# Splitting two output stores into 8-row transfers, and one group for the last four values of the last unit

## Chip, cores and metric

The kernel runs on one core of one Trainium2 chip. The metric is device time in microseconds (us), lower is better. Run-to-run spread is given beside each median.

## The reference

```python
batch, n_heads, seq, head_dim = 8, 12, 1024, 64
attn_weights: (8, 12, 1024, 1024) float32
v:            (8, 12, 1024, 64)   float32
out = np.einsum('bhqs,bhsd->bhqd', attn_weights, v)
```

Reading the weights in float32 is nearly all of the traffic: 402.7 MB of them, 25.2 MB of `v`, and 25.2 MB written.

## The kernel before

The 96 heads are worked off in 48 pairs ("units"). For each unit, GpSimd (POOL) issues one load of 128 rows that converts float32 to bf16 on the way. PE (the matmul engine) transposes the weights, multiplies by `v`, and transposes the result back; DVE (VectorE) and ACT (ScalarE) do the copies between; the output unit (128 rows of 4 KB) is stored by a transfer that POOL issues. Two weight buffers let the next load run during compute. The stores of the seven units before the last are held back and issued behind the last load ("held stores" below). Shortened, with comments of mine:

```python
def load_attn(ip):                       # one unit = 128 rows of 64 KB in float32
    abf = abf_pool.tile([P, G, S], bf16)             # two buffers
    for g0, gn in chunks_of.get(ip, [(0, G)]):       # last units: in parts
        last = nc.gpsimd.dma_start(out=abf[:, ds(g0, gn)]..., in_=attn_p[ip][...])

def store(ip, osb):
    nc.gpsimd.dma_start(
        out=out_p[ip].rearrange("p g d -> p (g d)"),     # 128 rows of 4 KB
        in_=osb.rearrange("p g d -> p (g d)"),
        single_packet=True,
    )

# the last unit: parts of 4, 4, 4, 2, 1 and 1 of its 16 values, each part
# transposed, multiplied, copied out, and stored on its own from SP
chunks_of[NP - 1] = [(0, 4), (4, 4), (8, 4), (12, 2), (14, 1), (15, 1)]
stores_of = {4: (0, 8), 8: (8, 4), 12: (12, 2), 15: (14, 2)}

# ... (transposes, multiplications and the copies between them are cut)
```

## Time and profile before

| | before |
|---|---|
| time, median of 4 runs | 1061.61 us (1061.13 to 1061.64) |
| span in the profile | 1059.6 us |
| DMA engines busy | 90% or more in 39 of 40 slices |
| PE busy | 76% |
| last load landed / last small store issued | 1048.6 / 1054.29 us |
| last held store, completion on its first / last DMA engine | 1050.1 / 1057.8 us |

From the page of the kernel before: the share of the span in 40 slices (tenths, so 9 is 90% or more), the DMA queues, the total of the memory traffic, and the chain that ended last.

```profile
DMA  9999999999999999999999999999999999999998
...
q0 software_dynamic: 18432, 238.03, 100.0%
q1 hardware_dynamic: 720, 1.57, 0.4%
q8 instruction: 44, 0.72, 0.2%
q14 instruction: 12, 0.10, 0.0%
HBM read 427.82 MB, written 25.17 MB: 428 GB/s over the span
...
DMA 73%; issue 14%; PE 9%; POOL 2%; ACT 1%; DVE 0%; POOLq 0%
```

The kernel is bound by DMA: the DMA engines have hardly any idle time to remove. q1 is the queue of the transfers that SP (SyncE) issues. q8 holds 44 packets of 16 KB (16384 bytes in the packet records) of the kind that the page calls instruction: 0.72 MB of 240 (the records count a 64 KB row of weights by the 32 KB that it writes as bf16), 0.2% of the time of 16 engines. The list of waits says the same from PE's side (columns: who waited for what, us in total, times, longest):

```profile
PE pt L150 <- DMA abf<-in_attn_weights_dram: 194.3, 49, 24.9
```

The trace keeps 16 landing times for every load of weights. I read them as one for each of the 16 DMA engines that the page counts; which engine a time belongs to is not recorded. They show what the 16-engine mean hides. Times in us after the first of the 16, sorted, for a load of weights (landing records of the trace, not a view of the page):

```
first landed at   the other engines behind it
  24.58   0.0 0.0 0.0 0.0 0.0 0.1 0.1 0.1 0.1 0.1 0.1 0.1 0.1 0.1 0.1 0.2
 220.41   0.0 0.0 0.1 0.1 0.2 0.4 0.4 0.6 1.3 1.3 1.3 1.3 1.4 1.4 1.6 1.9
 612.76   0.0 0.0 0.1 0.2 0.4 0.5 1.0 1.6 3.5 3.5 3.5 3.6 3.6 3.7 3.8 4.0
1035.53   0.0 0.1 0.1 0.2 0.4 0.8 1.8 2.8 5.8 5.8 5.8 5.9 6.0 6.9 7.1 7.3
```

Eight engines fall behind, in steps of about 1.1 us, one engine after another, at the times of the 16 KB instruction packets (for one, a delay of 1.4 us in the load first landed at 396.04 us is 2.4 in the load at 415.33, and a packet started at 411.6). What waits for a load waits for the slowest engine: of the load in the last row the first landing is at 1035.53 us and the last at 1042.86, and PE starts its transposes at 1042.99. So the time of this kernel is that of its slowest engine.

The end of the last unit, in the timeline of the kernel before (start us, duration us, engine and line, operation, count, and in brackets the idle time ahead and what ended it):

```profile
1042.95 11.67 SPq L266 DMA_DIRECT2D out_dram<-osb  x4
...
1042.99 2.17 PE L150 MATMUL pt<-ident,abf 128*128 128x128 f32 x16 [0.92 <-DMA abf<-in_attn_weights_dram]
...
1046.79 1.18 PE L150 MATMUL pt<-ident,abf 128*128 128x128 f32 x8
...
1049.33 0.70 PE L150 MATMUL pt<-ident,abf 128*128 128x128 f32 x4
...
1051.66 0.70 PE L150 MATMUL pt<-ident,abf 128*128 128x128 f32 x4
...
1053.15 0.62 PE L252 MATMUL px<-vbf,at 128*128 128x128 bf16 x8 [0.79 <-DVE at L159]
...
1054.06 0.21 ACT L263 COPY osb<-px 64x64 f32<-64x64 f32 x1 [1.74 <-DVE osb L263]
```

The last four values go through in three groups (8, 4 and 4 transposes), each waiting for its own copies.

### The profile page before, as it was taken

The page shows a single profiled execution, that of the slowest core. Times are in us where ns is not written, and L with a number is a line of the kernel's source. Part 1 is how long each engine was busy: PE and PEld are TensorE (multiplying, and loading weights), DVE is VectorE, ACT ScalarE, POOL GpSimd, SP SyncE. Part 2 cuts the span into 40 slices and gives each one's busy share as a digit, 9 for nine tenths or more (in the row PEclk, how much of TensorE's full clock was granted, in tenths as well). Part 3 has the DMA queues.
Part 4 walks back from the last instruction along what each step waited for, and adds up shares of the span by engine and source line. Part 5 has one row for each costly group of instructions (what it writes and reads, how often), then busy time and mean ns, then how long its engine had stood idle before and what let it go on. Part 6 is the DMA issues. An engine that isn't in the chain of part 4 may idle for free.

```text
span 1059.6 us, 12899 instructions
## 1 busy us (share of the span) xinstructions
PE 808.4 (76%) x5640; PEld 645.0 (61%) x5640; DVE 390.7 (37%) x590; ACT 399.6 (38%) x486; POOL 71.8 (7%) x137
## 2 busy tenths in 40 slices
PE   0988778876778767787687876888678776788996
PEld 0676567654666556665476655766557555676785
DVE  0443334433344333343334333343334333344443
ACT  0353334433344333344344333443334333343542
POOL 2000000000000000000000000000000000001011
PEclk9998878988888888788888887788889887788999
DMA  9999999999999999999999999999999999999998
GB/s 217 219 218 234 222 237 231 225 226 222 239 224 232 222 231 237 223 220 231 238 226 229 227 224 236 229 222 229 229 230 235 221 227 228 236 215 210 217 215 243
DMA packets 19208, 240.43 MB, mean 227 GB/s; under 512 B 2128, under 2 KB 2512, under 8 KB 11984
## 3 DMA queue, kind: packets, MB, share of 16 engines
q0 software_dynamic: 18432, 238.03, 100.0%
q1 hardware_dynamic: 720, 1.57, 0.4%
q8 instruction: 44, 0.72, 0.2%
q14 instruction: 12, 0.10, 0.0%
HBM read 427.82 MB, written 25.17 MB: 428 GB/s over the span
## 4 chain that ended last, share of the span: by engine, by line
DMA 73%; issue 14%; PE 9%; POOL 2%; ACT 1%; DVE 0%; POOLq 0%
DMA abf<-in_attn_weights_dram 73%; PE pt L150 5%; PE px L186 2%; ACT osb L194 1%; POOL vr L124 1%; POOL out_dram L203 1%; PE px L136 1%; PE px L252 1%; PE po L169 0%; DVE vbf L144 0%; POOL abf L108 0%; DVE at L159 0%; ACT at L159 0%; DVE osb L263 0%; ACT osb L263 0%
## 5 line engine op out<-in xcount | busy, mean ns | idle before, releaser
L150 PE MATMUL pt<-ident,abf 128*128 128x128 f32 x3072 | 463.2, 319 | 194.3 <-DMA abf<-in_attn_weights_dram 194.3
L150 PEld LDWEIGHTS pt<-ident,abf 128*128 128x128 f32 x3072 | 449.7, 214 | 209.4 <-issue 116.3
L159 DVE COPY at<-pt 128x1024 bf16<-128x1024 bf16 x480 | 319.5, 688 | 443.1 <-PE pt L150 441.7
L159 ACT COPY at<-pt 128x1024 bf16<-128x1024 bf16 x288 | 288.7, 1012 | 223.3 <-PE pt L150 129.2
L169 PE MATMUL po<-at,vbf 128*64 128x512 bf16 x1440 | 216.5, 391 | 0.0
L169 PEld LDWEIGHTS <-vbf 128*64 128x64 bf16 x1440 | 106.5, 108 | 92.9
L194 ACT COPY osb<-px 128x512 f32<-128x512 f32 x90 | 50.8, 587 | 154.9 <-PE px L186 151.5
L181 ACT COPY ot<-po 128x512 f32<-128x512 f32 x45 | 26.3, 585 | 191.4 <-PE po L169 191.4
L186 PE MATMUL px<-ident,ot 128*128 128x128 f32 x360 | 69.8, 340 | 30.3 <-DVE vbf L144 17.4
L186 PEld LDWEIGHTS px<-ident,ot 128*128 128x128 f32 x360 | 52.8, 174 | 50.7 <-DVE vbf L144 28.7
L144 DVE CAST vbf<-px 128x512 bf16<-128x512 f32 x48 | 33.2, 691 | 95.9 <-PE px L136 95.9
L181 DVE COPY ot<-po 128x512 f32<-128x512 f32 x45 | 31.1, 691 | 100.8 <-PE po L169 100.8
L136 PE MATMUL px<-vr,spread 32*128 32x512 bf16 x384 | 53.8, 386 | 18.5 <-DVE vbf L144 18.5
L108 POOL DMA_DIRECT2D abf<-in_attn_weights_dram x58 | 31.5, 546 | 512.5 <-PE pt L150 507.2
L203 POOL DMA_DIRECT2D out_dram<-osb x47 | 25.2, 536 | 462.8 <-ACT osb L194 424.8
L144 ACT CAST vbf<-px 128x512 bf16<-128x512 f32 x48 | 28.1, 585 | 63.7 <-PE px L136 63.7
L136 PEld LDWEIGHTS <-spread 32*128 32x128 bf16 x384 | 17.2, 93 | 52.5 <-issue 43.0
L252 PE MATMUL px<-vbf,at 128*128 128x128 bf16 x384 | 23.9, 219 | 2.3 <-ACT at L159 1.2
L252 PEld LDWEIGHTS <-at 128*128 128x128 bf16 x384 | 22.5, 98 | 3.1 <-DVE at L159 1.5
L263 ACT COPY osb<-px 64x256 f32<-64x256 f32 (+2 forms) x14 | 4.7, 337 | 20.6 <-DVE osb L263 20.6
L124 POOL DMA_DIRECT2D vr<-in_v_dram x23 | 12.4, 538 | 0.0
L263 DVE COPY osb<-px 64x256 f32<-64x256 f32 (+2 forms) x14 | 5.3, 378 | 18.4 <-PE px L252 18.4
(10 smaller groups left out, 6.1 us busy)
## 6 DMA issues: line engine op xcount, KB each, us to landing
abf<-in_attn_weights_dram POOLq DMA_DIRECT2D x44, 4096.0 KB, 33.2
out_dram<-osb POOLq DMA_DIRECT2D x47, 512.0 KB, 20.0
vr<-in_v_dram POOLq DMA_DIRECT2D x23, 512.0 KB, 21.4
abf<-in_attn_weights_dram POOLq DMA_DIRECT2D x4, 2048.0 KB, 25.6
abf<-in_attn_weights_dram POOLq DMA_DIRECT2D x7, 1024.0 KB, 27.3
v<-in_v_dram SPq DMA_DIRECT2D x1, 1024.0 KB, 4.7
abf<-in_attn_weights_dram POOLq DMA_DIRECT2D x1, 512.0 KB, 29.7
abf<-in_attn_weights_dram POOLq DMA_DIRECT2D x2, 256.0 KB, 30.1
```

Of the source, the lines that this page charges most:

```text
L108: last = nc.gpsimd.dma_start(out=abf[:, ds(g0, gn)].rearrange("p g s -> p (g s)"), in_=attn_p[ip][:, ds(g0 * S, gn * S)],)
L124: nc.gpsimd.dma_start(out=vr.rearrange("p b x -> p (b x)"), in_=v_g[iv])
L136: nc.tensor.matmul(out=px, lhsT=spread[rows, b], rhs=vr[rows, b], start=(b == 0), stop=(b == VB - 1),)
L144: copy(out=vbf[:, :, h % 2], in_=px.rearrange("p (k d) -> p k d", k=SB))
L150: nc.tensor.matmul(out=pt[:, k], lhsT=words[:, k], rhs=ident, is_transpose=True, start=(k == 0), stop=(k == KW - 1),)
L159: copy(out=at[:, g].rearrange("c k j two -> c (k j two)"), in_=pt.rearrange("c k j -> c (k j)").bitcast(bf16),)
L169: nc.tensor.matmul(out=po[h][ds(half * D, D)], lhsT=vbf[:, 2 * kw + par, h], rhs=at[:, ds(half * GH, GH), kw, ds(h * HP, HP), par], start= ...
L181: copy(out=ot[:, :, h], in_=po[h].rearrange("p (j q) -> p j q", j=GH))
L186: last = nc.tensor.matmul(out=px[:, j], lhsT=ot[:, j0 + j].rearrange("p h q -> p (h q)"), rhs=ident, is_transpose=True, start=(j == 0), st ...
L194: nc.scalar.copy(out=o_halves[:, :, ds(j0, jn)].rearrange("p half j d -> p j half d"), in_=px.rearrange("p j (half d) -> p j half d", half=2),
L203: nc.gpsimd.dma_start(out=out_p[ip].rearrange("p g d -> p (g d)"), in_=osb.rearrange("p g d -> p (g d)"), single_packet=True,)
L252: behind = nc.tensor.matmul(out=px[:, g - g0].rearrange("p h d -> p (h d)"), lhsT=at[:, g, kw, :, par], rhs=vbf[:, 2 * kw + par].rearrange ...
```

## The change

The intent: (1) move 8 rows of each of two stores away from the late DMA engines, by issuing them from SP in transfers of 8 rows, which the prediction assumes to run on eight engines only, the same ones each time ("these eight" in it; no run had shown it yet); (2) treat the last four values as one group, so that PE does not wait between them. The split stores also do without the `single_packet=True` of the store from POOL. In the cut below, the comment lines stand for code left out.

```diff
+    SHIFTED = (20, 30)
...
-    stores_of = {4: (0, 8), 8: (8, 4), 12: (12, 2), 15: (14, 2)}
+    stores_of = {4: (0, 8), 8: (8, 4), 12: (12, 4)}
...
     def store(ip, osb):
+        if ip in SHIFTED:
+            for p0 in range(0, P, 8):
+                rows = ds(p0, 8)
+                nc.sync.dma_start(
+                    out=out_p[ip][rows].rearrange("p g d -> p (g d)"),
+                    in_=osb[rows].rearrange("p g d -> p (g d)"),
+                )
+            return
         nc.gpsimd.dma_start(
...
-        for c0, cn in chunks_of[ip]:
-            for g0 in range(c0, c0 + cn, DG):
-                gn = min(DG, c0 + cn - g0)
-                # transpose gn values, then their matmuls, copies and store
+        for g0 in range(0, G, DG):
+            # transpose DG = 4 values, then their matmuls, copies and store
```

The loads of the last unit keep their parts; only the computation is regrouped.

More of the change, by code (lines that the diff above doesn't have):

```diff
@@ L240, in direct_pair @@
         osb = o_pool.tile([P, G, D], fp32)
-        for c0, cn in chunks_of[ip]:
-            for g0 in range(c0, c0 + cn, DG):
-                gn = min(DG, c0 + cn - g0)
-                with tc.issue_after(behind.ins):
-                    for g in range(g0, g0 + gn):
-                        transpose_g(abf, at, g)
-                px = px_pool.tile([P, gn, 2, D], fp32)
-                for g in range(g0, g0 + gn):
-                    n = 0
-                    for kw in range(KW):
-                        for par in range(2):
-                            behind = nc.tensor.matmul(
-                                out=px[:, g - g0].rearrange("p h d -> p (h d)"),
-                                lhsT=at[:, g, kw, :, par],
-                                rhs=vbf[:, 2 * kw + par].rearrange("p h d -> p (h d)"),
-                                start=(n == 0),
-                                stop=(n == SB - 1),
-                            )
-                            n += 1
-                for h in range(2):
-                    copy = nc.vector.tensor_copy if h == 0 else nc.scalar.copy
-                    rows = ds(h * HP, HP)
-                    copy(out=osb[rows, ds(g0, gn)], in_=px[rows, :, h])
-                if ip == NP - 1 and g0 in stores_of:
-                    gs = ds(*stores_of[g0])
-                    nc.sync.dma_start(out=out_p[ip][:, gs], in_=osb[:, gs])
@@ new lines, in direct_pair @@
+        for g0 in range(0, G, DG):
+            with tc.issue_after(behind.ins):
+                for g in range(g0, g0 + DG):
+                    transpose_g(abf, at, g)
+            px = px_pool.tile([P, DG, 2, D], fp32)
+            for g in range(g0, g0 + DG):
+                n = 0
+                for kw in range(KW):
+                    for par in range(2):
+                        behind = nc.tensor.matmul(
+                            out=px[:, g - g0].rearrange("p h d -> p (h d)"),
+                            lhsT=at[:, g, kw, :, par],
+                            rhs=vbf[:, 2 * kw + par].rearrange("p h d -> p (h d)"),
+                            start=(n == 0),
+                            stop=(n == SB - 1),
+                        )
+                        n += 1
+            for h in range(2):
+                copy = nc.vector.tensor_copy if h == 0 else nc.scalar.copy
+                rows = ds(h * HP, HP)
+                copy(out=osb[rows, ds(g0, DG)], in_=px[rows, :, h])
+            if ip == NP - 1 and g0 in stores_of:
+                gs = ds(*stores_of[g0])
+                nc.sync.dma_start(out=out_p[ip][:, gs], in_=osb[:, gs])
```

## The prediction

> **What bounds the kernel now.** DMA. The slice row shows the DMA engines 90% or more busy in every slice but the last. In the chain of waits the loads of the weights hold 73%; PE waits 194.3 us for them (list of waits). The DMA packet records show the engines back to back: a 64 KB row of weights every 2.41 us on each engine, a 4 KB store row every 0.155 us.
>
> So the time is the work of the *slowest* DMA engine plus what follows it. The 16 completion increments of every transfer show how far the engines are apart: 0.2 us at 25 us, then a growing split into two groups of eight. At the last transfers eight engines are within 2.8 us of the first, the other eight 5.8 to 7.3 us behind it. The jumps are about 1.1 us each and fall on one engine after another, with the 44 packets of 16 KB of the instruction queue (44/8 x 1.1 = 6 us). [...] The last held stores end at 1050 to 1053 us (leading eight) and 1056 to 1057.85 us (lagging), the final small store at 1058.04, the span at 1059.6.
>
> **The change.** (1) Two units' stores (512 KB each, 8 rows of 4 KB per engine) become 16 transfers of 8 rows each from SP. [...] These eight then carry 16 more rows and the others 16 fewer: 16 x 0.155 = 2.5 us each way, closing 5 of the 6 us. The 32 issues cost SP 0.33 us each, off the path. (2) In the last unit the last three groups (2+1+1 values) become one of 4: transposes 2.15 us, matmuls 1.95, copies 0.42 + 0.37 in sequence, one store fewer. Now, from 1046.8, they take until 1054.29 to issue the last store, PE waiting on copies.
>
> **On the critical path.** If the lagging eight are relieved, their loads land 2.5 us earlier, the last near 1046.1 instead of 1048.6; transposes end near 1046.8, matmuls near 1048.8, the last store issues near 1049.7 and is hidden behind held stores. These end near 1055.4 on the relieved engines, near 1055.8 on the slowest loaded one. Gain 2.0 to 2.5 us. The tail alone gains nearly nothing, because held stores end at 1057.85 anyway; it keeps compute out of the way.
>
> Which engine numbers lag the profile does not show; I infer from the change's size that its author knew. If they are the first eight (or mixed), the time rises by about 2.5 us, to near 1064.
>
> **Predicted: 1059.4 us**, range 1057.6 to 1062.0. Faster by over 2%: 0.005; within 2%: 0.985; slower: 0.01.
>
> **Right if:** completion spreads drop to about 3 us after the second split store; loads of the last unit land 2.5 us earlier; the last small store issues near 1050; per-packet times are unchanged; PE waits less than 0.9 us before each group of the last unit.
>
> **Wrong if:** the spread grows to about 11 us (wrong engines); interleaving two queues costs the loaded engines more than 0.155 us per row (32 rows at 0.1 us extra would eat the gain); or 8-row transfers use other engines.

## The result, and the profile after

| | before | after |
|---|---|---|
| time, median of 4 runs each | 1061.61 us (1061.13 to 1061.64) | 1063.09 us (1062.5 to 1064.03) |
| span in the profile | 1059.6 us | 1062.3 us |
| last small store issued | 1054.29 us | 1054.65 us |
| last held store, first / last engine | 1050.1 / 1057.8 us | 1052.6 / 1060.6 us |

The ratio is 1.0016 (95% interval 0.9998 to 1.0033), within 2%. Ratios here are taken over the fast runs; they are not quite the ratios of the medians quoted. The profiled run of the kernel after is its slowest (1064.03 us; the spans of its four runs are 1060.7 to 1062.3 us), while that of the kernel before (1061.36 us) is an ordinary one. So the traces show a wider gap, 2.7 us of span, than the medians, 1.5 us.

The answering lines of the page of the kernel after:

```profile
DMA  9999999999999999999999999999999999999997
...
q0 software_dynamic: 18144, 236.99, 99.5%
q1 hardware_dynamic: 1088, 2.62, 0.7%
q8 instruction: 44, 0.72, 0.2%
q14 instruction: 12, 0.10, 0.0%
HBM read 427.82 MB, written 25.17 MB: 426 GB/s over the span
...
DMA 73%; PE 12%; issue 11%; POOL 2%; ACT 1%; DVE 0%; POOLq 0%
```

The same bytes moved and the same 44 instruction packets; 1.05 MB went over from q0 to q1 as intended. q1's 1088 packets are the 720 of before, less 144 for the small store that fell away, plus 512 for the 32 new transfers: 16 each, 8 rows and 8 completions. Beside a record at its issue each has 8 landing times, where a load has 16 (the first: issue 488.4 us, landings 494.4 to 496.5). I read this as eight engines for each transfer. The last slice of DMA went from 8 to 7 tenths: fewer engines are busy at the end (of the last held store 14 of the 16 completions are in by 1055.7 us, the other two come at 1060.5 and 1060.6). The wait of PE for the loads grew (list of waits):

```profile
PE pt L153 <- DMA abf<-in_attn_weights_dram: 197.6, 50, 25.2
```

The end of the last unit in the timeline of the kernel after:

```profile
1045.61 9.37 SPq L275 DMA_DIRECT2D out_dram<-osb  x3
1045.63 2.17 PE L153 MATMUL pt<-ident,abf 128*128 128x128 f32 x16 [0.91 <-DMA abf<-in_attn_weights_dram]
...
1049.43 1.67 PE L153 MATMUL pt<-ident,abf 128*128 128x128 f32 x12
...
1051.26 0.72 PE L153 MATMUL pt<-ident,abf 128*128 128x128 f32 x4 [0.17 <-DMA abf<-in_attn_weights_dram]
...
1051.82 1.95 PE L261 MATMUL px<-vbf,at 128*128 128x128 bf16 x32
...
1054.26 0.37 ACT L272 COPY osb<-px 64x256 f32<-64x256 f32 x1 [2.11 <-DVE osb L272]
```

The regrouping does what it should: once the load of the last value is in, PE runs through. But the third group of four starts at 1045.63 instead of 1042.99 us, after the same 0.9 us wait for its load: every load of the last unit lands about 2.6 us *later*. The chain that ended last, cut to this part in order of time (start, us, what), starts the last four transposes only when their load is in:

```profile
1021.88 29.25 DMA abf<-in_attn_weights_dram
1051.13 0.14 issue
1051.26 0.72 PE pt L153 x4
1051.98 1.80 PE px L261 x32
```

The completions tell why. A late load of the kernel after, in the form used above:

```
1036.71   0.0 0.2 1.7 1.7 1.8 2.2 2.2 2.3 2.4 2.5 2.5 2.7 3.2 4.3 8.7 8.8
```

Of the 16 engines, twelve are now within 2.6 us of each other, much as intended. Two are in front, and **two are alone, 8.7 us behind the first** and 4.4 us behind the next.

### The profile page after: what moved, and what is told of

It is laid out like the page before. It is cut to its first block, busy times and chain, and to the rows that moved or that the text cites. A ratio compares the mean times of both kernels' runs of the same rounds, so it can differ in the third digit from the quotient of the medians.

```text
span 1062.3 us, 12933 instructions
## 1 busy us (share of the span) xinstructions
PE 807.4 (76%) x5640; PEld 644.8 (61%) x5640; DVE 391.0 (37%) x588; ACT 399.3 (38%) x484; POOL 70.0 (7%) x135
## 3 DMA queue, kind: packets, MB, share of 16 engines
q1 hardware_dynamic: 1088, 2.62, 0.7%
## 4 chain that ended last, share of the span: by engine, by line
DMA 73%; PE 12%; issue 11%; POOL 2%; ACT 1%; DVE 0%; POOLq 0%
DMA abf<-in_attn_weights_dram 73%; PE pt L153 8%; PE px L189 2%; ACT osb L197 1%; POOL vr L127 1%; PE px L139 1%; POOL out_dram L214 1%; PE px L261 1%; PE po L172 0%; POOL abf L111 0%; DVE vbf L147 0%; DVE osb L272 0%; ACT osb L272 0%; POOLq L214 0%; POOLq L81 0%
## 5 line engine op out<-in xcount | busy, mean ns | idle before, releaser
L272 ACT COPY osb<-px 64x256 f32<-64x256 f32 x12 | 4.4, 367 | 18.0 <-DVE osb L272 18.0
L272 DVE COPY osb<-px 64x256 f32<-64x256 f32 x12 | 5.0, 417 | 16.0 <-PE px L261 16.0
```

## Experiments

In the recorded expectations and below, "refilled" is only a name for an engine that falls behind with the instruction packets; the first eight are those that the transfers of 8 rows load. Theory A: the eight refilled engines are not the last eight; two of them are among the first eight, so these two got the split rows on top of the instruction packets. Rival B: the late ones are exactly the last eight, and two queues taking turns on an engine cost more than the rows themselves. Rival C: the new last unit costs the time.

### Numbering the engines: m1_marks

```diff
+    for k in range(2, 16):
+        for c in range(2):
+            nc.sync.dma_start(out=mark[ds(0, k)], in_=attn_p[0][ds(0, k), ds(c * 2048, 2048)])
```

This is the kernel before with small loads ("marks") of k rows of 8 KB added early, two for each k, into the buffer that held the first `v`. The numbers rest on an assumption of mine, which no trace shows directly: such a transfer puts one row on each of k engines, and a wider one adds engines to those of a narrower one. A number below is a place in this order, from 0; the trace records none. Under the assumption an engine's delay from the marks tells its number.

> Numbers the DMA engines. Early in the kernel before, SP loads k rows of 8 KB twice, for k = 2 to 15; if a transfer of k rows uses the k lowest-numbered engines, engine 1 (and 0) gets 28 rows, engine 2 26, ..., engine 14 2 and engine 15 none, so the completions of later transfers should lie about 0.6 us apart in engine order, in all about 8.6 us. Each later 16 KB instruction packet then moves one known engine by about 1.1 us. Theory A (the refilled eight are not the last eight; two of the first eight are refilled too): the jumps fall on eight engines of which exactly two are among 0 to 7. Theory B (the refilled eight are exactly the last eight and the split rows cost too much): all jumps fall on 8 to 15. Time some 8 to 10 us above the kernel before; that number is not the point.

Measured: correct, 1067.43 us (one run, 5.8 us above the kernel before, where 8 to 10 were expected). After the marks, each 16 KB instruction packet moves one engine. A part of the sorted delays of the transfers just before and after six such packets in a row, in us behind the first engine:

```
packet at   delays before it (a part)           after it
  299       4.3 4.4 5.0 6.3                     4.3 4.4 6.0 6.3      5.0 -> 6.0
  323       2.9 3.4 3.9 4.3                     2.9 3.4 4.3 ... 5.0  3.9 -> 5.0
  348       2.1 2.9 3.4 4.3                     2.2 2.9 4.3 ... 4.5  3.4 -> 4.5
  373       1.7 2.2 2.9 4.3                     1.7 2.1 4.0 4.3      2.9 -> 4.0
  395       1.7 2.1 4.0 4.3                     1.7 3.3 4.0 4.3      2.1 -> 3.3
  418       1.7 3.3 4.0 4.3                     3.0 3.3 4.1 4.3      1.7 -> 3.0
```

One engine moves each time by 1.0 to 1.3 us, although a packet itself is recorded as 0.89 to 0.98 us (87 of the 88 in the kernels before and after; one took 1.03). After eight packets the turn begins again. The two packets of this turn before these six (at 248 and 268 us) fall on the engines that the transfer at 242 us shows at 8.0 us (its packet counted) and at 6.2 us. In that transfer the first engine of the turn has taken two packets and the other seven one, at about 1.1 us each. Less these, the refilled engines stood at about 5.8, 5.2, 3.8, 2.8, 2.3, 1.8, 1.0 and 0.6 us of marks: the five smallest lie roughly one mark apart (engines 14 to 10), then comes a gap of one engine, then 8, another gap, then 6 and 5. The turn begins at 5 and ends at 14. The engine that stays in front is read as 15, the one without marks. I read the refilled ones as 5, 6, 8, 10, 11, 12, 13 and 14. The reading of 5, 6 and 8 is by size of a delay only, since the 8 KB instruction packets of q14, recorded as 0.32 us each within the span of the kernel before, may shift some engines too; so it is tested below for 5 and 6. The 3.8 us read as engine 8 lies midway between what 0.58 us a mark (5.8 us over ten marks) gives for engine 8, 4.1 us, and for engine 9, 3.5 us.

### Each part of the change alone: tail_only, shift_only

```diff
# tail_only: the kernel after with
-    SHIFTED = (20, 30)
+    SHIFTED = ()
# shift_only: the kernel before with
+    SHIFTED = (20, 30)     # and the new store()
```

> Only the last unit's change, no split stores. All theories of the DMA engines say the time is that of the kernel before within 0.5 us (1061.1 to 1061.6), because held stores end at the same 1057.9 us; the last small store issues near 1052, 2 us earlier than before. If the tail itself costs the 1.5 us, this run shows 1063.

Measured: 1061.59 us (1061.51 to 1061.86, 5 runs) against 1061.59 (1061.38 to 1062.48, 9 runs), ratio 0.9999 (0.9985 to 1.0013). The last small store did issue early, at 1052.4 instead of 1054.29 us. Rival C falls: the tail alone is worth nothing. The reason that the traces give is that the slowest DMA engines end no earlier: the last held store and the last small store end at 1057.8 and 1058.0 us in the kernel before, and at 1058.3 and 1057.9 us in tail_only.

> Only the two split stores, the old last unit. Theory A: two engines carry both burdens and end 2.5 us later than before, so 1063.0 to 1064.0 us, and the completion spread of the last loads has two engines some 9 us behind the first and two alone in front. Theory that the tail is to blame: 1059.5 to 1061.5.

Measured: 1062.80 us (1062.33 to 1065.34, 5 runs), ratio 1.0015 (1.0003 to 1.0028). The whole loss comes with the split stores. Its last held store ends at 1060.1 and 1060.4 us on two engines, while the other fourteen end by 1055.9 (the profiled run took 1063.77 us, the second slowest of five).

### Which engines may be loaded: k5_one, k6_one, k7_one

```diff
# the kernel after with
-    SHIFTED = (20, 30)
+    SHIFTED = (20,)
+    ROWS = 5              # k6_one: 6, k7_one: 7
...
-            for p0 in range(0, P, 8):
-                rows = ds(p0, 8)
+            for p0 in range(0, P, ROWS):
+                rows = ds(p0, min(ROWS, P - p0))
```

If 5 and 6 are the two refilled engines among the first eight, and k rows go to the first k engines, transfers of 5 rows (engines 0 to 4) load none of them, 6 rows one, 7 rows two.

> As the change, but one unit's store (20) alone, in transfers of 5 rows (the last of 3). From the numbered engines I read the refilled eight as 5, 6, 8, 10, 11, 12, 13, 14. Theory A then says no refilled engine is loaded: engines 0 to 4 carry about 17.6 more rows (2.7 us), all others 8 fewer (1.24 us), so the eight late ones end at about 1056.6 us instead of 1057.85 and no pair stands apart; time 1060.3 to 1060.8, about 1.0 us below the kernel before. If instead splitting a store costs time of itself (two queues taking turns, more descriptors), the time is at or above the kernel before.

Measured: 1060.41 us (1059.95 to 1060.88, 5 runs) against 1061.81 (1061.57 to 1062.32, 9 runs), ratio 0.9988 (0.9974 to 1.0001). No run of it was as slow as any of the kernel before. The interval only just reaches 1, and 0.1% is small: the direction rests on this separation of the runs and on the trace below, not on the interval.

> The same with 6 rows (the last of 2): engine 5 joins the loaded ones, which carry 13.3 more rows (2.1 us). Theory A: exactly one engine, refilled and loaded, stands alone at the end, about 2.1 us later than the last one of the kernel before (near 1059.9 in the trace); time 1062.5 to 1063.5. If the refilled ones among the first eight are other than 5 and 6 (say 6 and 7), this run is as fast as the one with 5 rows.

Measured: 1062.22 us (1062.01 to 1064.01, 5 runs), ratio 1.0009 (0.9996 to 1.0021); the median is 0.3 us under the range expected, two of five runs are above 1063. Its trace is of one of these two (1063.35 us). By its interval it is not clearly slower than the kernel before, but every run of it is slower than every run of k5_one.

> As with 6 rows, now 7 (18 transfers of 7, one of 2): settles whether the second refilled engine among the first eight is 6 or 7. Each loaded engine gets about 10 more rows (1.6 us). Engine 6: two completions stand apart at the end of the last held store; engine 7: still one. The marked run says two.

Measured: one run, 1063.20 us. It was run on another chip. On two engines the last held store ends apart from the rest (below).

The times of completion of the last held store on its 16 engines, in us, sorted (landing records of each trace, rounded):

```
before      50.1 50.1 50.1 50.3 50.5 50.7 51.8 53.1 56.3 56.3 56.3 56.4 57.4 57.5 57.6 57.8   +1000
after       52.6 52.9 52.9 52.9 53.3 53.4 53.4 53.6 53.7 53.8 54.3 54.4 55.0 55.7 60.5 60.6   +1000
shift_only  52.4 52.5 52.9 53.3 53.4 53.5 53.5 53.6 53.6 53.6 54.6 55.4 55.6 55.9 60.1 60.4   +1000
k5_one      48.6 49.1 49.3 53.3 53.5 53.8 55.1 55.1 55.2 55.2 55.2 55.8 56.1 56.3 56.5 56.5   +1000
k6_one      51.9 52.1 52.6 52.8 53.0 53.1 54.4 55.1 55.1 55.3 55.3 55.3 55.9 57.1 57.4 59.8   +1000
k7_one      51.8 51.8 52.0 52.2 52.2 52.6 53.6 54.6 54.8 54.8 55.0 55.0 55.9 56.1 58.8 59.7   +1000
```

With 5 rows no engine stands apart at the end, with 6 rows one (59.8), with 7 rows two, with 8 rows two. This is theory A's count each time, and it settles engines 5 and 6, in the assumed numbering: if each row more loads one engine more, the counts (0, 1, 2 and 2) say that the sixth and the seventh engine to be loaded were late already; the first five and the eighth were not. The last completion in k5_one is 1056.5 where 1056.6 was expected, and in k6_one 1059.8 where 1059.9 was expected.

Rival B is not needed for any of these counts, though a small cost of splitting remains. In the kernel after, the two double-loaded engines end at 1060.5 and 1060.6 us. The two that end last in the kernel before are at 1057.6 and 1057.8; if these are engines 5 and 6, they lost 2.8 to 2.9 us, and 16 rows of 0.155 us make 2.5. The rest fits the packet records: 180 of the 256 split rows are recorded at 0.172 us, where most rows of POOL's stores have 0.159, which makes about 0.3 us over the 32 rows of an engine. The relieved engines gain what they should too (57.4 to about 55.0).

The timeline of k5_one's last unit answers to the one of the kernel after; again the last four transposes wait for their load:

```profile
1045.26 1.67 PE L154 MATMUL pt<-ident,abf 128*128 128x128 f32 x12
...
1047.11 0.72 PE L154 MATMUL pt<-ident,abf 128*128 128x128 f32 x4 [0.18 <-DMA abf<-in_attn_weights_dram]
```

They start at 1047.11 us against 1051.26 in the kernel after. In these traces the last load is ready for PE 4.15 us earlier when one store is moved to five engines that have slack than when two are moved to eight of which two have none. The traces are of k5_one's fastest run and the other's slowest; the medians differ by 2.7 us.

### Dose, and the tail once more: k5_two, k5_oldtail

```diff
# k5_two: k5_one with
+    SHIFTED = (20, 30)
# k5_oldtail: k5_one's split store in the kernel before, with its old last unit
```

> Two stores in 5 rows, the new last unit: the dose. Engines 0 to 4 carry 35 more rows than before (5.5 us), the refilled eight 16 fewer (2.5 us, ending near 1055.3). Of the unrefilled engines the latest ended at 1053.1 in the kernel before; if it is one of 0 to 4 it ends near 1058.6, so 1061.8 to 1062.6: worse than one store, at the level of the kernel before or a little above, and the late ones are now loaded ones without refills. If relief of the refilled engines were all that counts, 1059.2.

Measured: 1062.82 us (1062.68 to 1062.84, 5 runs) against 1061.53, ratio 1.0011 (0.9997 to 1.0025). It was run on another chip. The last held store ends at 1059.2 us (expected 1058.6), and the end is spread (56.6, 57.2, 58.3, 59.2) instead of two alone: by the expectation's count of rows, the late ones are now the loaded engines without instruction packets. Relief of the refilled engines is not all that counts; the maximum over all engines is.

> One store in 5 rows, with the last unit of the kernel before. Its last small store would issue about 1.2 us earlier than before, near 1053, and end near 1056.8, about when the held stores end (1056.5): 1060.4 to 1061.0, at most 0.5 us above the same with the new last unit (1060.4). If the new last unit was needed, 1061 or more.

Measured: 1060.42 us (1060.25 to 1060.70, 5 runs), ratio 0.9989 (0.9977 to 1.0002); k5_one had 1060.41 in the other set of rounds, on another chip (1.1 and 1.4 us below the kernel before beside each). So the new last unit was not needed even when the DMA engines end earlier: in this run the last small store ends at 1057.2 and the held stores at 1057.0 us.

k5_one and k5_oldtail are the versions that came out below both kernels, below the kernel before by 1.4 and 1.1 us of medians. Every run of each is below every run of the kernel before beside it, but both intervals just reach 1.

## Why the prediction was wrong

The prediction was 1059.4 us (1057.6 to 1062.0); measured 1063.09, outside the range and on the other side of the kernel before.

- **The bound** (DMA, and in it the slowest engine) held: the loads end about 2.6 us later with the same bytes moved, and the two engines that stand apart are the ones that set this end.
- **The step that failed:** "If the lagging eight are relieved, their loads land 2.5 us earlier." The prediction said that the profile did not show which engine numbers lag, and that "I infer from the change's size that its author knew". That inference failed. The last load landed at 1051.1 us, not at the 1046.1 forecast and later than the 1048.6 of the kernel before. Six of the lagging eight were relieved; two, engines 5 and 6, were among those loaded. The assumption that k rows go to the first k engines fits every run (5, 6, 7 and 8 rows gave 0, 1, 2 and 2 stragglers); what was guessed was which engines fall behind with the instruction packets.
- **One straggler is enough.** The last load of the kernel after has its first landing at 1041.7 us and its last at 1051.1, and the last four transposes start at 1051.26, after the last. Twelve engines came together as planned, and two stragglers gave the time. Worse, engines 5 and 6 begin each turn of the instruction packets (as read from the marks), and 44 packets over eight engines give the first four of the turn six packets and the others five: these two were among the last already.
- **The fallback** was right in direction and cause: "If they are the first eight (or mixed), the time rises by about 2.5 us, to near 1064." In the profile the span rose by 2.7 us and the profiled run took 1064.03 us; the median rose by 1.5 us. So 2.5 us is the size in the slowest run, which happens to be the profiled one, and too much for the median. The spread of the late loads was 8.8 to 9.9 us; the prediction named about 11 for the wrong engines. I gave this case too small a chance.
- **Sizes:** "16 x 0.155 = 2.5 us each way" held for the relieved engines (about 2.4 us) and roughly for the loaded ones (2.8 to 2.9 us); interleaving cost a few tenths at most. "Completion spreads drop to about 3 us" held for twelve engines only.
- **The tail:** "The tail alone gains nearly nothing" was right (0.9999). The store was to issue near 1049.7; it issued at 1054.65, because the load it needs landed at 1051.1 instead of 1046.1. That it "keeps compute out of the way" was not borne out: k5_oldtail is as fast without it.

Left open: the kernels whose stragglers are refilled engines scatter more (after 1062.5 to 1064.0, shift_only 1062.3 to 1065.3, k6_one 1062.0 to 1064.0) than k5_one (0.9 us) or k5_two, whose stragglers are not (0.2 us). The place of the last instruction packets may be what differs from run to run, but only one run of each kernel has a trace. That 8 and not 9 is among the refilled engines is read from the marks alone. No run issues a store from SP without splitting it, so what the change of queue does by itself is not measured.

## What to carry to other kernels

When every DMA engine is busy to the end, look at the 16 completions of a transfer, not at the mean: here the slowest engine set the time, and the completions of one load, 0.2 us apart at the start, were 7.3 us apart at the end of the kernel before, split by packets that are 0.2% of the engines' time. Before work is moved between engines, number them: a few small transfers of known width, early in a scratch run, gave an order here that the runs with 5, 6, 7 and 8 rows bore out for engines 5 and 6. Then load only engines that have slack, and no more than that slack: a second store moved to the same five engines (k5_two) took back more than the first had gained.
